# A decoder block on one core: tile-by-tile waits for reused bytes, and value loads queued behind the exchanged queries

## The chip, the cores and the metric

The kernel runs on one core of a Trainium2 chip. The metric is the device time of one execution in microseconds (us); three runs of the kernel before took 944.96, 946.88 and 947.32 us, so the median is 946.88 us.

## The reference

The block normalizes `x` (1024 positions by 1024 channels, float32), projects it with `w_in`, runs two causal attentions side by side, multiplies each with a SiLU gate, projects both back, merges them with sigmoid gates, applies `w_out`, a second RMS norm and the residual.

```python
h = rms_norm(x, g_pre); proj = h @ w_in            # qa ka va fa za | qb kb vb zb | gates
ya = fox_attention(qa, ka, va, log_sigmoid(fa + b_forget))   # 8 heads of 64, decay by cumulated log_f
yb = diff_attention(rope(qb), rope(kb), vb, lam)             # 4 heads, 2 score maps of 64, values of 128
ya = ya * silu(za);  yb = rms_norm(yb, g_subln) * (1 - lam_init) * silu(zb)
merged = sigmoid(gate_a) * (ya @ w_branch[0]) + sigmoid(gate_b) * (yb @ w_branch[1])
out = x + rms_norm(merged @ w_out, g_post)
```

## The kernel before

Matmuls run on float32 operands that are split in a rounded high part and a low remainder, so one product is two or three matmuls. The work has four stages in the program's order.

- **Values first.** The eight row blocks of `x` are normalized and transposed into `hT`; all value projections (`v_block`) and the forget gates are computed, split, and written to device memory (`va_d`, `vb_d`).
- **Attention, eight units.** Units 0 to 3 are the four differential heads, units 4 to 7 pairs of forgetting heads. `unit_proj(u)` makes four tasks, each a 128x512 projection of 24 matmuls (`project`, L246): k and q, each in two chunks, named `pk` and `pq`. In units 0 to 3 every chunk goes through `rope`: ACT copies the PSUM tile to `raw` (L283), SP issues four DMAs that swap 32-row bands into `sw` (L287; `swk`, `swq`), DVE multiplies and adds (L288, L290), POOL multiplies the swapped copy (L289). `stack` then makes the stacked operands `TA`, `TB`, `KA`, `KB` with two ACT casts (L295, L297) and two DVE subtractions (L296, L298). `swapped` (L407) fetches, for a group of two query blocks, the half-exchanged queries `X0` and `X1` by two DMAs each. `s_row` makes a row of scores: matmuls with the stacked queries (L421) and with the exchanged ones (L422), into one of three PSUM buffers, and DVE reduces each piece (L423), which frees the buffer. ACT takes the exponential (L428), POOL scales and adds (L512, L515). `av` transposes the probabilities (L450), splits them (L453, L454) and multiplies with the values (L474).
- **How units overlap.** While unit u runs its scores, the projections of unit u+1, the gate projections `z` and other small tasks are its filling work. The projections have two PSUM buffers (`pj`). The values of a unit are one load of 1 MB (`V`, L495) into one of two buffers; `load()` stands at the start of the unit.
- **Gates, merge, output.** `h_load` fetches eight 1 MB tiles `T`, `gates_plain` and `gates_pair` compute the merge gates, `branch` and `merge` the two back projections, `out_pair` the output.

A scheduler sets the order of the instructions on each engine from the program's order as priority, from the dependences, and from modelled durations. Every engine then runs its own list in order. All DMAs stand in the one list of SP, which stops at the first DMA that has to wait. Pools are memory areas: a pool opened over the bytes of a closed one has to wait for them.

Of the kernel before, what the change touches and what calls it, by code (L numbers as in the profile page):

```python
# [21 lines left out]
CH = 512  # L22
# [19 lines left out]
def f32(ap):  # L42
    return ap.bitcast(F32)
# [3 lines left out]
def tile_hybrid_block(  # L47
# [18 lines left out]
    nc = tc.nc  # L66
# [41 lines left out]
    t_d = {m: [dram.tile([P, 4, CH], F32, name=f"t_d{m}_{part}") for part in range(2)]  # L108
           for m in (4, 5, 6, 7)}
# [139 lines left out]


    with ExitStack() as st:
        qk = st.enter_context(tc.tile_pool(name="qk", bufs=2))
        pp = st.enter_context(tc.tile_pool(name="pp", bufs=6))
        ptp = st.enter_context(tc.tile_pool(name="ptp", bufs=3))
        stg = st.enter_context(tc.tile_pool(name="stg", bufs=2))
        pj = st.enter_context(tc.tile_pool(name="pj", bufs=2, space=PSUM))
        sps = st.enter_context(tc.tile_pool(name="sps", bufs=3, space=PSUM))
        tps = st.enter_context(tc.tile_pool(name="tps2", bufs=2, space=PSUM))
        yps = st.enter_context(tc.tile_pool(name="yps", bufs=1, space=PSUM))

        nc.sync.dma_start(gsub, g_subln.rearrange("o p -> p o"))
        nc.gpsimd.tensor_scalar(gsub, gsub, 1.0 - LAM_INIT, 1.0, op0=ALU.mult, op1=ALU.mult)
# [138 lines left out]
        def swapped(T, m, g, nm):  # L401

            src = T["TB" if m else "TA"]
            qs = slice(2 * g * P, (2 * g + 2) * P)
            t = qk.tile([P, 2 * P], F32R, tag=f"X{m}", name=f"X{m}{nm}_{g}", bufs=3)
            for a, b in ((UPR, DNR), (DNR, UPR)):
                nc.sync.dma_start(f32(t[a]), f32(src[b, qs]))  # L407
            return t

        def s_row(T, m, i, X, bias, boff, nm):  # L410

# [73 lines left out]
        def unit_attn(u, T):  # L485

            diff = u < 4
            t = u if diff else u - 4
            vt = qk.tile([P, NB, 256], F32R, tag="V", name=f"V{u}")
            src = (vb_d if diff else va_d)[:, t, :].rearrange("(b p) c -> p b c", p=P)  # L490
            cb = []
            groups = []

            def load():
                nc.sync.dma_start(f32(vt), src)  # L495
# [36 lines left out]
            else:  # L532
# [25 lines left out]
                for g in GORD[u]:  # L558
                    for m in range(2):
# [4 lines left out]
                            lambda m=m, g=g, rows=rows: av(  # L564
                                rows, g, vt, m * P, True, evac(m, g), f"f{u}_{m}_{g}",
                                u == 7 and g in FING)))
            return load, groups


        lt = pp.tile([P, 4, 64], F32, tag="P", name="lt")  # L570
# [43 lines left out]
        T, tasks = unit_proj(0)  # L614
        for tk in tasks:
            tk()
        pend = None
        for u in range(8):
            load, groups = unit_attn(u, T)
            if u == 1:  # L620
                forget_sums()
            load()
            fill = []
            if u + 1 < 8:
                T, tasks = unit_proj(u + 1)
                fill += tasks
            for t in ZFILL[u]:
                fill += z_tasks(t)
            fill[2:2] = [lambda k=k: h_combinations(k) for k in TFILL[u]]
            for t in SFILL[u]:  # L630
                fill += [lambda t=t, c=c: sum_squares(t, c) for c in range(2)]
                fill.append(lambda t=t: subln_scales(t))
            total = sum(s[0] for s in groups)
            done, nf = 0, 0
            for n, (wgt, rws, prd) in enumerate(groups):
                for r in rws:
                    r()
# [14 lines left out]


    gw = ExitStack()
    wx = gw.enter_context(tc.tile_pool(name="wx", bufs=2))
    tmp = gw.enter_context(tc.tile_pool(name="tmp", bufs=8))
    ydp = gw.enter_context(tc.tile_pool(name="ydp", bufs=1))
    xst = ExitStack()
    xps = xst.enter_context(tc.tile_pool(name="xps", bufs=8, space=PSUM))

    def split(dst, src, eng=nc.vector):

# [82 lines left out]


    tst = ExitStack()
    tpool = tst.enter_context(tc.tile_pool(name="tpool", bufs=1))

    yz = {}  # L750

# [36 lines left out]
             for m, (kh, sh) in hB.items()}  # L788

    def h_load():  # L790
        for m in (4, 6, 5, 7):
            ts = [tpool.tile([P, 4, CH], F32R, tag=f"T{m}{part}", name=f"T{m}{part}")
                  for part in range(2)]
            for part in range(2):
                nc.sync.dma_start(f32(ts[part]), t_d[m][part])
            h_ops[m] = [[t[:, k, :] for k in range(4)] for t in ts]

    def gates_pair(d, order):
        raw = []
# [19 lines left out]
    tst.close()  # L819


    mpool = gw.enter_context(tc.tile_pool(name="mpool", bufs=1))
# [205 lines left out]
```

## Time and profile before

| what | value |
|---|---|
| median of three runs | 946.88 us |
| the profiled execution: its time / its span | 945.37 us / 943.3 us |
| PE busy | 895.5 us, 95% of the span |
| DVE, ACT, POOL busy | 625.4, 435.8, 489.3 us |
| mean granted clock of TensorE | 0.988 |
| values first / attention / the rest, from the span's start | about 0 to 113, 113 to 603, 603 to 943 us |

The page gives busy times per engine; a table of stretches gives them for any part of the span, with the granted clock (1.00 is full speed) and what the DMA engines moved. Rows of the timeline start with the start and the duration in us; in brackets stands how long the engine was idle before and what ended that. "pk", "pq", "Sd" and so on are names of tiles without their numbers.

### The profile page before, as it was taken

The numbers are of one execution on the slowest core, as the hardware profiler recorded it, in microseconds if no ns is written. First come the engines' busy times: TensorE is split into PE (matmuls) and PEld (weight loads), VectorE is DVE, ScalarE is ACT, GpSimd is POOL, SyncE is SP. The second block draws the span as 40 slices with busy tenths as digits, with TensorE's granted clock in tenths as the row PEclk, the third lists the DMA queues.
The fourth block names the chain that finished last, engine by engine and source line by source line (L and its number), as shares of the span: only waits on it lengthen the run. The fifth ranks groups of instructions, "written<-read, shape, count | busy, mean of one in ns | idle before, by whom it ended". The sixth has DMA issues, their size and how long they took to land. (4 is left out here: it accounts for less than half of the span.)

```text
span 943.3 us, 13785 instructions
## 1 busy us (share of the span) xinstructions
PE 895.5 (95%) x4600; PEld 750.5 (80%) x4600; DVE 625.4 (66%) x1180; ACT 435.8 (46%) x862; POOL 489.3 (52%) x461
## 2 busy tenths in 40 slices
PE   7999989999999999999999998899999999999993
PEld 5899868787887888888878887788888888887872
DVE  6731248988767778577767558515868893559766
ACT  3421115575656766465755648524443450324331
POOL 7200024446546448364554566407667436878963
PEclk9999999999999999999999999999999999999997
DMA  9532354424316163444542442496556596211332
GB/s 312 186 129 90 118 151 121 110 74 120 108 42 196 43 181 126 123 125 138 167 151 74 135 151 92 152 404 234 174 176 196 165 351 222 72 40 46 105 118 89
DMA packets 118664, 136.95 MB, mean 145 GB/s; under 512 B 10545, under 2 KB 84273, under 8 KB 117570
## 3 DMA queue, kind: packets, MB, share of 16 engines
q1 hardware_dynamic: 118594, 136.08, 45.6%
q8 instruction: 36, 0.59, 0.3%
q14 instruction: 34, 0.28, 0.1%
HBM read 85.65 MB, written 37.81 MB: 131 GB/s over the span
## 5 line engine op out<-in xcount | busy, mean ns | idle before, releaser
L195 PE MATMUL pv<-wvhi,hT 128*128 128x264 f32 (+2 forms) x384 | 89.6, 326 | 0.4 <-DVE hT L181 0.4
L246 PE MATMUL pk<-hT,hi_k 128*128 128x512 f32 x256 | 84.8, 404 | 4.0 <-DVE KB L298 2.2
L246 PE MATMUL pz<-hT,hi_z 128*128 128x512 f32 x256 | 84.3, 396 | 0.0
L246 PE MATMUL pq<-hT,hi_q 128*128 128x512 f32 x256 | 82.8, 397 | 0.0
L713 PE MATMUL x_o<-wo_op,a_o 128*128 128x512 f32 x336 | 77.9, 391 | 3.6 <-POOL a_o L665 2.3
L846 PE MATMUL pb<-yT,hi_br 128*128 128x512 f32 x256 | 78.5, 389 | 0.0
L713 PEld LDWEIGHTS x_o<-wo_op,a_o 128*128 128x128 f32 x336 | 62.7, 188 | 18.7 <-POOL a_o L665 3.7
L713 PE MATMUL x_g<-T,a_g 128*128 128x512 f32 x336 | 77.5, 389 | 0.0
L713 PEld LDWEIGHTS x_g<-T,a_g 128*128 128x128 f32 x336 | 63.1, 188 | 13.1
L195 PEld LDWEIGHTS pv<-wvhi,hT 128*128 128x128 f32 x384 | 64.7, 191 | 6.3 <-DVE hT L181 0.7
L542 POOL TENSOR_SCALAR Pf<-Pf,lf 128x1024 f32<-128x1024 f32 (+3 forms) x64 | 52.5, 822 | 30.6 <-DVE lf L430 27.5
L428 ACT ACTIVATE Pf<-Pf,mxf 128x1024 f32<-128x1024 f32 (+3 forms) x64 | 49.7, 777 | 31.3 <-DVE mxf L423 28.8
L428 ACT ACTIVATE Pd<-Pd,mxd 128x128 f32<-128x128 f32 (+7 forms) x64 | 49.5, 774 | 30.8 <-DVE mxd L423 29.1
L538 POOL TENSOR_TENSOR cb<-cb,trim 128x128 f32<-128x128 f32 x64 | 30.2, 474 | 61.8 <-DVE mxf L423 44.2
L195 PE MATMUL pv<-wvlo,hT 128*128 128x512 f32 (+2 forms) x192 | 61.9, 325 | 0.0
L512 POOL TENSOR_SCALAR Pd<-Pd,ld 128x128 f32<-128x128 f32 (+7 forms) x32 | 25.5, 798 | 69.7 <-DVE ld L511 37.8
L246 PEld LDWEIGHTS pk<-hT,hi_k 128*128 128x128 f32 x256 | 48.3, 193 | 14.5 <-DVE KB L298 2.4
L713 PE MATMUL x_g<-hT,a_g 128*128 128x512 f32 x252 | 58.6, 389 | 0.0
L454 DVE TENSOR_TENSOR plf<-ptf,phf 128x512 fp32r<-128x512 f32 (+1 forms) x80 | 49.6, 633 | 10.4 <-ACT phf L453 9.8
L846 PEld LDWEIGHTS pb<-yT,hi_br 128*128 128x128 f32 x256 | 48.1, 188 | 10.0
L713 PEld LDWEIGHTS x_g<-hT,a_g 128*128 128x128 f32 x252 | 47.3, 188 | 9.8
L246 PEld LDWEIGHTS pq<-hT,hi_q 128*128 128x128 f32 x256 | 47.5, 189 | 8.9
(248 smaller groups left out, 2424.4 us busy)
## 6 DMA issues: line engine op xcount, KB each, us to landing
t_d<-t SPq DMA_DIRECT2D x32, 256.0 KB, 2.2
T<-t_d SPq DMA_DIRECT2D x8, 1024.0 KB, 14.9
raw<-in_w_in_dram SPq DMA_DIRECT2D x14, 512.0 KB, 4.1
vb_d<-vbs SPq DMA_DIRECT2D x8, 512.0 KB
va_d<-vas SPq DMA_DIRECT2D x8, 512.0 KB, 3.7
raw_k<-in_w_in_dram SPq DMA_DIRECT2D x8, 512.0 KB, 5.3
raw_q<-in_w_in_dram SPq DMA_DIRECT2D x8, 512.0 KB
V<-vb_d SPq DMA_DIRECT2D x4, 1024.0 KB
```

Of the source, the lines that this page charges most:

```text
L195: nc.tensor.matmul(ps[n], lhsT=hT[hp][k // 4][i // 4][:, k % 4, hs], rhs=wt[k][:, a:b], start=first, stop=(k == KT - 1 and hp == 1))
L246: nc.tensor.matmul(ps, lhsT=a[:, k, :], rhs=hT[h][k // 4][c][:, k % 4, :], start=(k == 0 and a is hi and h == 0), stop=(k == KT - 1 and a ...
L428: nc.scalar.activation(pr[:, 0:n], pr[:, 0:n], AF.Exp, bias=mx[:, len(pcs) - 1:len(pcs)], scale=-1.0, accum_out=le)
L454: nc.vector.tensor_tensor(pl[:, 0:n], pt[:, 0:n], ph[:, 0:n], op=ALU.subtract)
L512: nc.gpsimd.tensor_scalar(p2[:, 0:n], p2[:, 0:n], l2, 1.0, op0=ALU.mult, op1=ALU.mult)
L538: nc.gpsimd.tensor_tensor(diag, diag, trim, op=ALU.add)
L542: nc.gpsimd.tensor_scalar(p1[:, 0:n], p1[:, 0:n], l1, 1.0, op0=ALU.mult, op1=ALU.mult)
L713: nc.tensor.matmul(x[m], lhsT=a[:, ai, k, :], rhs=right[m][bi][k], start=(k == 0 and n == 0), stop=(k == 3 and n == 2))
L846: nc.tensor.matmul(ps, lhsT=a[:, kk, :], rhs=yT[g][h][:, k % 2, sl], start=(k == 0 and a is hi and h == 0), stop=(k == 3 and a is lo))
```

## The change

Three things are changed together.

1. The pools of attention and of what follows are opened with `reuse_waits="tile"`: where such a pool lies over the bytes of a closed one, each of its tiles waits only for the tiles that held its own bytes, and no longer for the whole closed pool. Several pools are laid from the other end of the memory (`side="right"`).
2. `h_load` allocates its tiles in the order 6, 4, 7, 5 and loads them in the order 4, 6, 5, 7 as before.
3. The load of a unit's values leaves `load()`. `load_v` is put in the list `vload`, and `swapped` issues it right behind the first DMA pair it makes after that: for unit 0 behind its first `X0`, for each later unit behind the first exchanged queries that are fetched once half of the groups of the unit before it have been traced.

```diff
-        qk = st.enter_context(tc.tile_pool(name="qk", bufs=2))
-        pp = st.enter_context(tc.tile_pool(name="pp", bufs=6))
...
+        qk = st.enter_context(tc.tile_pool(name="qk", bufs=2, reuse_waits="tile"))
+        pp = st.enter_context(tc.tile_pool(name="pp", bufs=6, side="right", reuse_waits="tile"))
...
+        pj = st.enter_context(tc.tile_pool(name="pj", bufs=2, space=PSUM, reuse_waits="tile"))
...
             for a, b in ((UPR, DNR), (DNR, UPR)):
-                nc.sync.dma_start(f32(t[a]), f32(src[b, qs]))
+                lastx[0] = nc.sync.dma_start(f32(t[a]), f32(src[b, qs])).ins
+            if vload:
+                with tc.issue_after(lastx[0]):
+                    vload.pop(0)()
             return t
+
+        lastx, vload = [None], []
...
+            def load_v():
+                nc.sync.dma_start(f32(vt), src)
+
             def load():
-                nc.sync.dma_start(f32(vt), src)
...
-            return load, groups
+            return load, load_v, groups
...
+        nxt = None
         for u in range(8):
-            load, groups = unit_attn(u, T)
+            load, load_v, groups = nxt or unit_attn(u, T)
+            nxt = None
+            if u == 0:
+                vload.append(load_v)
...
             for n, (wgt, rws, prd) in enumerate(groups):
+                if n == len(groups) // 2 and u < 7:
+                    nxt = unit_attn(u + 1, T)
+                    vload.append(nxt[1])
...
-    xps = xst.enter_context(tc.tile_pool(name="xps", bufs=8, space=PSUM))
+    xps = xst.enter_context(tc.tile_pool(name="xps", bufs=8, space=PSUM, reuse_waits="tile"))
...
-    tpool = tst.enter_context(tc.tile_pool(name="tpool", bufs=1))
+    tpool = tst.enter_context(tc.tile_pool(name="tpool", bufs=1, reuse_waits="tile"))
...
     def h_load():
+
+        ts = {m: [tpool.tile([P, 4, CH], F32R, tag=f"T{m}{part}", name=f"T{m}{part}")
+                  for part in range(2)] for m in (6, 4, 7, 5)}
         for m in (4, 6, 5, 7):
-            ts = [tpool.tile([P, 4, CH], F32R, tag=f"T{m}{part}", name=f"T{m}{part}")
-                  for part in range(2)]
             for part in range(2):
-                nc.sync.dma_start(f32(ts[part]), t_d[m][part])
-            h_ops[m] = [[t[:, k, :] for k in range(4)] for t in ts]
+                nc.sync.dma_start(f32(ts[m][part]), t_d[m][part])
+            h_ops[m] = [[t[:, k, :] for k in range(4)] for t in ts[m]]
```

In the changed kernel the lines L421 to L454 become L426 to L459, the value load L495 becomes L500, and the `T` loads L795 become L810. No instruction is added or taken out. The order of the engines differs from shortly before the attention to the first groups of unit 4, then is the same up to the seam at the gates, where the DMAs stand in another order. Three places follow.

**SP, the start of unit 0, before.** `V0` and `V1` are the values of units 0 and 1, `raw_q1` a weight load of 0.5 MB for unit 1, `swk0_0` and `swq0_0` the band swaps of unit 0's first chunks.

```order
L211 DMA va_d_97<-vas7_1116 128x1024
L572 DMA lt_1160<-in_lambda_q2_dram 128x64
L572 DMA lt_1160<-in_lambda_k2_dram 128x64
L495 DMA V0_1345<-vb_d_96 128x8x256
L495 DMA V1_1912<-vb_d_96 128x8x256
L228 DMA raw_q1_1514<-in_w_in_dram 128x8x128
L287 DMA swk0_0_1210<-rawk0_0_1208 32x512 x4
L287 DMA swq0_0_1255<-rawq0_0_1253 32x512 x4
L287 DMA swk0_1_1294<-rawk0_1_1292 32x512 x4
L407 DMA X0d0_0_1351<-TA0_1173 64x256 x2
L407 DMA X1d0_0_1354<-TB0_1174 64x256 x2
L287 DMA swq0_1_1333<-rawq0_1_1331 32x512 x4
```

The same place in the changed kernel:

```order
L211 DMA va_d_97<-vas7_1116 128x1024
L228 DMA raw_q1_1514<-in_w_in_dram 128x8x128
L287 DMA swk0_0_1210<-rawk0_0_1208 32x512 x4
L287 DMA swq0_0_1255<-rawq0_0_1253 32x512 x4
L287 DMA swk0_1_1294<-rawk0_1_1292 32x512 x4
L407 DMA X0d0_0_1350<-TA0_1173 64x256 x2
L500 DMA V0_1345<-vb_d_96 128x8x256
L407 DMA X1d0_0_1354<-TB0_1174 64x256 x2
L287 DMA swq0_1_1333<-rawq0_1_1331 32x512 x4
```

`V0` has moved from ahead of the first swaps to between `X0` and `X1` of unit 0's first group; `V1` stands eight rows below, between `X0` and `X1` of the third group and ahead of `swq1_0`. The four small loads `lt` stand about ten rows higher. The loads of the later units stand where they stood, within four rows.

**DVE, the second half of unit 0, before.** `lo_z0` is the low part of a gate weight, `TA1` a stacked query of unit 1, L423 the reduction of a piece of scores (listed as ISA).

```order
L290 TENSOR_TENSOR rawq1_0_1545<-rawq1_0_1545,swq1_0_1547 128x512
L423 ISA Pd0_0_4_1565,mxd0_0_4_1566<-Sd0_0_4_1_1571,dmask_1157,mxd0_0_4_1566 128x256
L423 ISA mxd0_0_4_1566 128x1
L236 TENSOR_TENSOR lo_z0_1853<-raw_z0_1850,hi_z0_1852 128x1024
L296 TENSOR_TENSOR TA1_1347<-rawq1_0_1545,TA1_1347 64x512
L423 ISA Pd0_1_4_1578,mxd0_1_4_1579<-Sd0_1_4_0_1580,dmask_1157 128x384
```

In the changed kernel (L428 is the reduction there):

```order
L296 TENSOR_TENSOR TA1_1346<-rawq1_0_1545,TA1_1346 64x512
L298 TENSOR_TENSOR TB1_1347<-rawq1_0_1545,TB1_1347 64x512
L428 ISA Pd0_0_4_1567,mxd0_0_4_1568<-Sd0_0_4_1_1573,dmask_1157,mxd0_0_4_1568 128x256
L428 ISA mxd0_0_4_1568 128x1
L236 TENSOR_TENSOR lo_z0_1855<-raw_z0_1852,hi_z0_1854 128x1024
L435 RECIPROCAL ld0_1_3_1489<-ld0_1_3_1489 128x1
L435 RECIPROCAL ld0_0_4_1577<-ld0_0_4_1577 128x1
L518 TENSOR_TENSOR ld0_1_3_1489<-ld0_1_3_1489,nlam_83 128x1
L428 ISA Pd0_1_4_1580,mxd0_1_4_1581<-Sd0_1_4_0_1582,dmask_1157 128x384
```

`TA1` now stands ahead of the reduction before `lo_z0`, so that between two reductions of scores `lo_z0` is the one long operation left. On PE, the same shift has put more filling work ahead: before the first score matmul of unit 1 stand 3 matmuls of unit 2's first projection in the kernel before, and 17 in the changed one.

**PE, the seam at the gates, before** (with what each row waits for; `pg` is the first gate projection):

```order
L474 MATMUL ypf_1_0_6860<-phf_1_0_0_6862,V_6170 128x256 [waits Activation_49]
L474 MATMUL ypf_1_0_6860<-plf_1_0_0_6863,V_6170 128x256 [waits DVE_49]
L474 MATMUL ypf_1_0_6860<-phf_1_0_0_6862,V_6170 128x128
L474 MATMUL ypf_1_0_6860<-plf_1_0_0_6863,V_6170 128x128
L246 MATMUL pg_0_0_6923<-hT_88,hi_g_0_6919 128x512 [waits DVE_49]
```

In the changed kernel:

```order
L479 MATMUL ypf_1_0_6860<-phf_1_0_0_6862,V_5934 128x256 [waits Activation_49]
L479 MATMUL ypf_1_0_6860<-plf_1_0_0_6863,V_5934 128x256 [waits DVE_49]
L479 MATMUL ypf_1_0_6860<-phf_1_0_0_6862,V_5934 128x128
L479 MATMUL ypf_1_0_6860<-plf_1_0_0_6863,V_5934 128x128
L246 MATMUL pg_0_0_6923<-hT_88,hi_g_0_6919 128x512
```

The first gate matmul has lost its wait for DVE. On SP, the eight `T` loads stand there ahead of four `yd` loads and two loads of `x`, and before behind them.

More of the change, by code (lines that the diff above doesn't have):

```diff
@@ L251, in tile_hybrid_block @@
     with ExitStack() as st:
-        qk = st.enter_context(tc.tile_pool(name="qk", bufs=2))
-        pp = st.enter_context(tc.tile_pool(name="pp", bufs=6))
[L254 to L259, printed above, removed]
+        qk = st.enter_context(tc.tile_pool(name="qk", bufs=2, reuse_waits="tile"))
+        pp = st.enter_context(tc.tile_pool(name="pp", bufs=6, side="right", reuse_waits="tile"))
+        ptp = st.enter_context(tc.tile_pool(name="ptp", bufs=3, side="right", reuse_waits="tile"))
+        stg = st.enter_context(tc.tile_pool(name="stg", bufs=2, side="right", reuse_waits="tile"))
+        pj = st.enter_context(tc.tile_pool(name="pj", bufs=2, space=PSUM, reuse_waits="tile"))
+        sps = st.enter_context(tc.tile_pool(name="sps", bufs=3, space=PSUM, reuse_waits="tile"))
+        tps = st.enter_context(tc.tile_pool(name="tps2", bufs=2, space=PSUM, reuse_waits="tile"))
+        yps = st.enter_context(tc.tile_pool(name="yps", bufs=1, space=PSUM, reuse_waits="tile"))
         nc.sync.dma_start(gsub, g_subln.rearrange("o p -> p o"))
@@ L654, in tile_hybrid_block @@
     gw = ExitStack()
-    wx = gw.enter_context(tc.tile_pool(name="wx", bufs=2))
-    tmp = gw.enter_context(tc.tile_pool(name="tmp", bufs=8))
-    ydp = gw.enter_context(tc.tile_pool(name="ydp", bufs=1))
+    wx = gw.enter_context(tc.tile_pool(name="wx", bufs=2, side="right", reuse_waits="tile"))
+    tmp = gw.enter_context(tc.tile_pool(name="tmp", bufs=8, side="right", reuse_waits="tile"))
+    ydp = gw.enter_context(tc.tile_pool(name="ydp", bufs=1, side="right", reuse_waits="tile"))
     xst = ExitStack()
-    xps = xst.enter_context(tc.tile_pool(name="xps", bufs=8, space=PSUM))
+    xps = xst.enter_context(tc.tile_pool(name="xps", bufs=8, space=PSUM, reuse_waits="tile"))
     def split(dst, src, eng=nc.vector):
@@ L819, in tile_hybrid_block @@
     tst.close()
-    mpool = gw.enter_context(tc.tile_pool(name="mpool", bufs=1))
+    mpool = gw.enter_context(tc.tile_pool(name="mpool", bufs=1, reuse_waits="tile"))
     mg = mpool.tile([P, KT, S], F32, name="mg")
```

## The prediction

> **What bounds the kernel now.** I read the page's first part, then a table of stretches, then the waits of PE and the timeline around them.
>
> ```profile
> span 943.3 us, 13785 instructions
> PE 895.5 (95%) x4600; PEld 750.5 (80%) x4600; DVE 625.4 (66%) x1180; ACT 435.8 (46%) x862; POOL 489.3 (52%) x461
> ```
>
> PE is busy for 895.5 of 943.3 us. An order change removes no matmul, so only PE's idle 47.8 us and slow-clock time can be won. The stretches say where they lie.
>
> ```profile
> core 0: us, PE busy (x) PEld busy (x) DVE busy (x) ACT busy (x) POOL busy (x), PEclk, DMA share, GB/s
> 134.00:139.00 5.00, 1.19 (x5) 0.66 (x5) 4.88 (x6) 3.17 (x6) 0.70 (x1) 1.00 0.20 50
> 139.00:146.00 7.00, 7.00 (x28) 5.77 (x27) 6.74 (x10) 1.54 (x3) 2.95 (x3) 0.76 0.35 86
> 146.00:168.00 22.00, 21.71 (x105) 17.36 (x104) 18.71 (x43) 13.65 (x33) 12.14 (x13) 1.00 0.48 117
> 168.00:174.00 6.00, 4.09 (x13) 3.23 (x13) 5.87 (x15) 3.06 (x7) 1.30 (x2) 0.72 0.30 70
> 174.00:200.00 26.00, 25.52 (x136) 21.45 (x134) 23.95 (x50) 17.02 (x30) 16.24 (x12) 1.00 0.45 121
> 200.00:310.00 110.00, 104.57 (x557) 86.98 (x558) 84.07 (x208) 66.75 (x138) 55.94 (x46) 1.00 0.38 105
> 604.00:930.00 326.00, 320.32 (x1404) 262.96 (x1404) 211.39 (x224) 114.99 (x192) 206.79 (x141) 1.00 0.54 180
> ```
>
> Two stretches stand out: 134 to 139, where PE works 1.19 of 5 us, and 168 to 174. Behind each stop the granted clock is low (0.76 over 7 us, 0.72 over 6 us), so a stop is paid twice. After 604 PE works 320.32 of 326 us; what PE gains earlier is kept there. The timeline of PE gives the stops, and the seam at the gates.
>
> ```profile
> 128.25 0.39 PE L246 MATMUL pk<-hT,lo_k 128*128 128x512 f32 x1
> ...
> 133.69 0.39 PE L246 MATMUL pq<-hT,lo_q 128*128 128x512 f32 x1
> 135.84 0.70 PE L246 MATMUL pk<-hT,hi_k 128*128 128x512 f32 x2 [1.76 <-ACT rawk L283]
> 138.59 0.51 PE L246 MATMUL pk<-hT,lo_k 128*128 128x512 f32 x1 [2.04 <-DVE lo_k L236]
> ...
> 170.02 0.49 PE L421 MATMUL Sd<-KA,TA 128*128 128x256 f32 x1 [1.91 <-DVE mxd L423]
> ...
> 603.91 0.74 PE L246 MATMUL pg<-hT,hi_g 128*128 128x512 f32 x2 [0.91 <-DVE ys L552]
> ```
>
> Why PE stops at 134 is read backwards through four engines.
>
> ```profile
> 114.67 1.41 SPq L495 DMA_DIRECT2D V<-vb_d  x2
> 117.87 2.37 SPq L228 DMA_DIRECT2D raw_q<-in_w_in_dram  x1
> 120.33 4.68 SPq L287 DMA_DIRECT2D swk<-rawk  x4
> ...
> 130.16 0.69 DVE L288 TENSOR_TENSOR rawk<-rawk,cosT 128x512 f32<-128x512 f32 x1 [8.77 <-DMA swk<-rawk]
> 130.20 1.80 POOL L289 TENSOR_TENSOR swk<-swk,sinT 128x512 f32<-128x512 f32 x1 [19.21 <-DMA swk<-rawk]
> 133.83 0.62 ACT L295 CAST KA<-rawk 64x512 fp32r<-64x512 f32 x1 [10.01 <-DVE rawk L290]
> 135.11 0.59 ACT L283 COPY rawk<-pk 128x512 f32<-128x512 f32 x1
> ```
>
> The four swaps of the first k chunk are issued from 120.33 and have landed only at 130.16. DVE stands idle 8.77 us. ACT waits for the rotated chunk until 133.83, and behind its two casts in ACT's list stands the copy at 135.11 that empties the PSUM buffer PE needs next. Then DVE, late too, delays `lo_k` and PE once more. What held the swaps is the traffic ahead of them:
>
> ```profile
> 122.00:124.00 2.00, 2.00 (x11) 1.65 (x10) 0.00 (x0) 0.59 (x1) 0.00 (x0) 1.00 1.09 346
> 126.00:128.00 2.00, 2.00 (x10) 1.67 (x9) 0.00 (x0) 0.00 (x0) 0.00 (x0) 1.00 1.04 160
> ```
>
> First the two value loads (2.1 MB) at some 346 GB/s, 6.1 us; then `raw_q` (0.52 MB, pieces of 512 bytes) at some 160 GB/s, 3.3 us. The DMA engines are full in both.
>
> **The change part by part.**
>
> *Values behind the queries.* V0 and V1 leave the place ahead of `raw_q`. The swaps still follow `raw_q`, whose issue at 117.87 waits for DVE, not for V. What they then need:
>
> ```profile
> raw_k<-in_w_in_dram SPq DMA_DIRECT2D x8, 512.0 KB, 5.3
> ...
> swk<-rawk SPq DMA_DIRECT2D x32, 64.0 KB, 2.0
> ```
>
> ```profile
> 123.23 0.59 ACT L283 COPY rawq<-pq 128x512 f32<-128x512 f32 x1 [2.23 <-PE pq L246]
> ...
> 133.22 1.49 POOL L234 TENSOR_SCALAR hi_k<-raw_k 128x1024 fp32r<-128x1024 f32 x1
> ...
> 135.72 2.41 SPq L287 DMA_DIRECT2D swk<-rawk  x4
> ...
> 137.32 1.22 DVE L236 TENSOR_TENSOR lo_k<-raw_k,hi_k 128x1024 fp32r<-128x1024 f32 x1
> ```
>
> A weight load of this size takes 5.3 us from issue to landing, so `raw_q` lands at 123.2 and the swaps behind it at about 124.5 (estimate) instead of 130.16: 5.7 us earlier. The rotation takes 3.7 us as before (130.16 to 133.83), so ACT is free for the next copy when its chunk is done (PE's row at 128.25), over 4 us before PE asks at 133.9. The q swaps are issued once ACT has copied their chunk at 123.8, 2.4 us for four, and land 2.0 later, 128.3; POOL needs 1.8 for them and 1.5 for `hi_k`, DVE 1.2 for `lo_k`: 132.8, against 134.3 when PE asks. So the first stop goes: 5.00 − 1.19 = 3.81 us idle, and 7.00 × (1 − 0.76) = 1.7 us of slow clock. Sum 5.5 us, close to DVE's head start of 5.7. Bounds: nothing if `raw_q` alone holds the swaps, 5.7 if DVE's head start reaches PE whole. I take 5.5.
>
> *The second stop.* DVE is the late one here:
>
> ```profile
> 165.35 2.31 DVE L236 TENSOR_TENSOR lo_z<-raw_z,hi_z 128x1024 fp32r<-128x1024 f32 x1 [0.54 <-POOL hi_z L234]
> 167.70 1.67 DVE L296 TENSOR_TENSOR TA<-rawq,TA 64x512 fp32r<-64x512 f32 x1
> 169.40 0.56 DVE L423 CUSTOM_DVE_ANT_0 Pd<-Sd,dmask 128x384 f32<-128x384 f32 x1
> ```
>
> `lo_z` and `TA` together keep DVE 4.05 us from the reduction that frees a score buffer. In the new order `TA` stands ahead of the reduction before, so 1.67 of the 1.91 us go by order alone, and DVE comes 5.7 us early. If the stop goes, so does the slow clock, 6.00 × (1 − 0.72) = 1.7 us: 3.6 us. Lower bound 0, since DVE is busy 18.71 of 22 us before it and may be late again. I take 3.6.
>
> [...]
>
> *The price of the new place.* V0 (1 MB, 3.0 us at 346 GB/s) now passes ahead of `X1` of the first group and of the second chunk's q swaps, V1 ahead of `X1` of the third group. By the times above `X0` is issued at about 133, V0 ends at 139.6, `X1` lands at 140, the swaps at 140.7. In PE's new order 24 + 9 projection matmuls stand ahead of the first product with `X1`; at 0.23 us each (326 us / 1404 in the gates) PE reaches it at 142. DVE waits for the swaps a microsecond or so, with PE's filling work as cover. So 0; if the cover is short, up to 3.0 us per load and the clock behind it.
>
> *What is given back.* DVE's own work is unchanged, and 14 more filling matmuls stand ahead of unit 1's first scores: 14 × 0.23 = 3.2 us of cover used early. In units 0 to 3 PE still idles 5.4 us (200 to 310) and mostly for DVE's reductions:
>
> ```profile
> PE Sd L421 <- DVE mxd L423: 4.0, 9, 1.0
> ```
>
> (174 to 385: 4.0 us in nine waits, longest 1.0.) From unit 4 on the order is the same, so nothing is won or lost there. Between 0 and 3.2 I take half, 1.6 us.
>
> *Tile-by-tile waits.* At the seam the first gate matmul no longer waits for the last DVE result: 0.9 us (row at 603.91). The eight T loads can start some 7 us earlier, but PE runs full from 604 on, so they are worth 0. At the first seam the long wait of the page,
>
> ```profile
> POOL hi_k L234 <- DMA vb_d<-vbs: 48.3, 1, 48.3
> ```
>
> belongs to a pool that is not changed and is covered by the value projections: 0. The `lt` loads move off DVE's list, where they only fill its idle time: 0. Issue costs: the same number of DMAs.
>
> *Sum:* 5.5 + 3.6 + 0.9 − 1.6 = 8.4 us. Against the profiled execution, 945.4 us (span 943.3 and 2.1 around it), that is 937.0; against the median of the runs, 946.9, it is 938.5. I predict 938.
>
> **The rivals.**
>
> - *DVE takes most of it back.* The first stop goes, but the second stays and the whole 3.2 us are given back: −5.5 − 0.9 + 3.2 = −3.2, about 943. For it: DVE busy 23.95 of 26 us after 174. Against it: the new place of `TA`.
> - *The values now stop PE (slower).* `X1` and the swaps behind V0 and V1 come after PE's cover is used up. Each such stop costs 3.0 us and, as behind the 1.91 us stop, 1.7 us of clock: 2 × 4.7 = 9.4. With the second stop left as it is: −5.5 − 0.9 + 9.4 = +3.0, about 949.5. It decides from the point where the first `X1` lands later than about 142 in today's time. For it: the swaps at 130.16 came only after everything issued ahead of them. [...] Against it: 2 us of margin, and a single load instead of two.
> - *The first stop doesn't go,* since `raw_q` with its 512-byte pieces still stands ahead of the swaps: only the 0.9 us of the seam, about 946. Against it: the 6.1 us that V took by the rate.
> - *More is won:* half of the waits in 200 to 310 go too, nothing is given back: 8.4 + 1.6 + 2.7 = 12.7, about 933.5.
>
> **How the numbers follow.** Chances: forecast 0.60 (its own range 934 to 941), DVE takes back 0.20, values stop PE 0.08, no first stop won 0.08, more won 0.04. The range has to leave out at most 0.2: 932 to 945 holds the forecast, the DVE rival and the larger gain, and leaves out 0.16. Three tenths of a per cent is about what a measurement of this kernel can tell from no change, here 2.8 us, so "faster" is below 944.0. Faster: 0.60 + 0.04 + 0.12 of the DVE rival = 0.76; same: 0.08 + 0.08 = 0.16; slower 0.08.
>
> **What would show it.** In the changed kernel's profile the first `swk` lands near 124, ACT's copy of the second k chunk ends before 131, PE has no stop over 1 us between 113 and 145 and the clock stays 1.00 there. No stop by L428 over 1 us with a low clock behind it around 160. The first `pg` follows the last `ypf` without a gap, at about 595 to 596. T is issued at about 594 to 600. I am wrong if PE stops for `X1` (L427) or if stops for L428 in units 0 to 3 sum to more than 8 us.

## The result, and the profile after

The changed kernel takes 937.73 us (median of 4 runs, 936.16 to 939.74), the kernel before in the same session 947.1 us (4 runs). The ratio is 0.9905, 95% interval 0.9878 to 0.9932: faster by 9.4 us, beyond what counts as no change. A second session, shown below, gave 0.9919 (0.9900 to 0.9938). Slow executions are left out of all medians: there is one, of 1102 us at a clock of 0.85, in the experiment with one more load. The profiled execution took 938.31 us, 7.06 less than the profiled one before. The head of its page:

```profile
span 936.2 us, 13774 instructions
PE 891.2 (95%) x4600; PEld 746.8 (80%) x4600; DVE 627.0 (67%) x1180; ACT 437.1 (47%) x862; POOL 493.6 (53%) x461
```

The table of stretches of the changed kernel, with the columns shown before (length, busy time and count of PE, PEld, DVE, ACT, POOL, then PE's granted clock, the DMA share, GB/s):

```profile
134.00:139.00 5.00, 4.49 (x22) 3.58 (x21) 4.80 (x6) 1.24 (x2) 1.48 (x2) 1.00 0.42 124
139.00:146.00 7.00, 6.25 (x29) 4.96 (x28) 2.82 (x7) 1.37 (x4) 1.78 (x1) 1.00 0.71 192
146.00:168.00 22.00, 20.57 (x94) 15.52 (x94) 19.17 (x52) 14.80 (x33) 12.06 (x12) 1.00 0.67 174
168.00:174.00 6.00, 5.74 (x30) 4.73 (x28) 5.26 (x5) 2.21 (x4) 5.81 (x5) 1.00 0.59 155
174.00:200.00 26.00, 22.25 (x114) 17.86 (x115) 22.37 (x52) 15.55 (x27) 13.07 (x9) 1.00 0.31 84
200.00:310.00 110.00, 107.48 (x584) 90.69 (x584) 89.75 (x222) 71.44 (x152) 58.87 (x49) 1.00 0.39 107
```

The hole at 134 to 139 (PE 1.19 of 5 us before) is nearly closed and the clock is full through 174. But 174 to 200, where PE was busy for 25.52 us, now has 22.25. PE's timeline of the changed kernel shows which waits are left. The number in square brackets is the idle time ahead of the row.

```profile
136.16 0.30 PE L426 MATMUL Sd<-KB,TB 128*128 128x128 f32 x1 [0.51 <-DVE TB L298]
142.64 0.30 PE L427 MATMUL Sd<-KB,X1d 128*128 128x128 f32 x1 [0.75 <-DMA X1d<-TB]
...
163.09 0.50 PE L426 MATMUL Sd<-KA,TA 128*128 128x512 f32 x1 [0.84 <-DVE mxd L428]
...
176.34 0.44 PE L426 MATMUL Sd<-KA,TA 128*128 128x384 f32 x1 [0.82 <-DVE mxd L428]
...
199.50 0.60 PE L615 MATMUL ft<-ident,fs 128*8 128x128 f32 x4 [1.77 <-DVE fs L606]
...
595.37 0.27 PE L479 MATMUL ypf<-plf,V 128*128 128x128 f32 x1
595.48 0.68 PE L246 MATMUL pg<-hT,hi_g 128*128 128x512 f32 x2
```

No stop between 113 and 146 is longer than 0.75 us; what stops PE now are reductions (at 163, 174, 176 and 193) and the transposes of the forget gates (`ft`, fed by `fs`); the first gate matmul `pg` follows the last value product without a gap. SP's queue and DVE in the changed kernel, for the chain that the prediction followed backwards:

```profile
116.11 0.38 SPq L228 DMA_DIRECT2D raw_q<-in_w_in_dram  x1
117.37 2.53 SPq L287 DMA_DIRECT2D swk<-rawk  x4
...
134.59 1.15 SPq L407 DMA_DIRECT2D X0d<-TA  x2
135.79 0.58 SPq L500 DMA_DIRECT2D V<-vb_d  x1
136.46 1.22 SPq L407 DMA_DIRECT2D X1d<-TB  x2
137.78 2.44 SPq L287 DMA_DIRECT2D swq<-rawq  x4
```

```profile
121.51 0.69 DVE L288 TENSOR_TENSOR rawk<-rawk,cosT 128x512 f32<-128x512 f32 x1 [5.43 <-DMA swk<-rawk]
128.32 0.69 DVE L288 TENSOR_TENSOR rawq<-rawq,cosT 128x512 f32<-128x512 f32 x1 [2.15 <-DMA swq<-rawq]
...
143.44 0.69 DVE L288 TENSOR_TENSOR rawq<-rawq,cosT 128x512 f32<-128x512 f32 x1 [3.00 <-DMA swq<-rawq]
```

The first k swaps land at 121.51 instead of 130.16. The second q swaps, now behind V0, let DVE wait 3.00 us.

How far the changed kernel is ahead at the same point of the work, from the timelines of PE (start of the row; "again" is the second profiled execution of the same kernel, from the last set of runs below):

| point | before | changed | again | lead |
|---|---|---|---|---|
| first `pq` | 116.66 | 116.55 | 116.05 | 0.1 / 0.6 |
| last `ypd` (end of unit 3) | 383.88 | 378.64 | 376.81 | 5.2 / 7.1 |
| the stop at `pk` by `KB` | 489.98 | 483.37 | 481.16 | 6.6 / 8.8 |
| last `ypf` | 602.73 | 595.37 | 592.11 | 7.4 / 10.6 |
| first `pg` | 603.91 | 595.48 | 592.22 | 8.4 / 11.7 |
| span | 943.3 | 936.2 | 932.2 | 7.1 / 11.1 |

At the last `ypd` the two kernels have not done the same work: PE has 1979 matmuls behind it in the changed kernel and 1972 in the kernel before. Seven matmuls at 364.51 / 1972 = 0.185 us are 1.3 us, so the lead in work is nearer 6.5 and 8.4 us there, and it hardly changes from there to the stop at `pk`.

### The profile page after: what moved, and what is told of

Its sections match the earlier page's. It is cut to its first block, busy times and chain, and to the rows that moved or that the text cites. A ratio compares the mean times of both kernels' runs of the same rounds, so it can differ in the third digit from the quotient of the medians.

```text
span 936.2 us, 13774 instructions
## 1 busy us (share of the span) xinstructions
PE 891.2 (95%) x4600; PEld 746.8 (80%) x4600; DVE 627.0 (67%) x1180; ACT 437.1 (47%) x862; POOL 493.6 (53%) x461
## 5 line engine op out<-in xcount | busy, mean ns | idle before, releaser
L246 PE MATMUL pk<-hT,hi_k 128*128 128x512 f32 x256 | 81.1, 394 | 2.0 <-DVE KB L298 2.0
L549 POOL TENSOR_SCALAR Pf<-Pf,lf 128x1024 f32<-128x1024 f32 (+3 forms) x64 | 50.4, 790 | 28.3 <-DVE lf L435 23.9
L459 DVE TENSOR_TENSOR plf<-ptf,phf 128x512 fp32r<-128x512 f32 (+1 forms) x80 | 49.8, 634 | 10.9 <-ACT phf L458 10.2
```

The source lines that it names most:

```text
L246: nc.tensor.matmul(ps, lhsT=a[:, k, :], rhs=hT[h][k // 4][c][:, k % 4, :], start=(k == 0 and a is hi and h == 0), stop=(k == KT - 1 and a ...
L459: nc.vector.tensor_tensor(pl[:, 0:n], pt[:, 0:n], ph[:, 0:n], op=ALU.subtract)
L549: nc.gpsimd.tensor_scalar(p1[:, 0:n], p1[:, 0:n], l1, 1.0, op0=ALU.mult, op1=ALU.mult)
```

## The experiments

The theory was: the value loads' place makes the gain, by way of the swaps and DVE; the pools add the seam; what is lost again in units 0 to 3 is DVE's lateness. The rivals: the tile-by-tile waits carry the gain; `raw_q`, not the values, holds the swaps (see *V0 at the front*); the losses come from POOL or from the place of `fs`. Each set of four ran on one chip beside the kernel before, whose medians were 944.64, 943.54 and 943.94 us.

### The values alone, the pools alone

*The values alone.* To the kernel before, only `load_v`, `vload` and `issue_after` are added; pools and `T` stay as they were:

```diff
+            if vload:
+                with tc.issue_after(lastx[0]):
+                    vload.pop(0)()
...
             def load():
-                nc.sync.dma_start(f32(vt), src)
```

> Only the value loads are moved; every pool and the T tiles are as before. Theory (the place of the value loads makes the gain, the pools add only the seam at the gates): the order on PE up to the gates is that of the changed kernel, so the first k swaps land near 121.5, PE has no stop over 1 us between 113 and 146, and the first gate matmul again starts about 0.9 us behind the last value product. Time about 1 us over the changed kernel: 938 to 940, ratio 0.991 to 0.993. Rival (the tile-by-tile waits of the unit pools carry part of it): a stop over 1 us is back before 174, ratio 0.995 or more.

Measured: 938.45 us, ratio 0.9924 (0.9905 to 0.9944). The first k swaps land at 122.79, PE idles 0.33 us in 113 to 146, and the seam is there again. PE's timeline of this kernel:

```profile
161.51 0.50 PE L426 MATMUL Sd<-KA,TA 128*128 128x512 f32 x1 [1.46 <-DVE mxd L428]
...
198.69 0.60 PE L615 MATMUL ft<-ident,fs 128*8 128x128 f32 x4 [2.58 <-DVE fs L606]
...
596.86 0.74 PE L246 MATMUL pg<-hT,hi_g 128*128 128x512 f32 x2 [0.91 <-DVE ys L559]
```

The values make most of the gain, 944.64 − 938.45 = 6.2 us. The rival's sign, a stop over 1 us ahead of 174, was there too (1.46 us), but without its price.

*The pools alone.* The changed kernel with the value loads back in `load()`:

```diff
             def load():
+                load_v()
...
-            if u == 0:
-                vload.append(load_v)
...
-                    nxt = unit_attn(u + 1, T)
-                    vload.append(nxt[1])
```

> All pools and the T tiles as in the changed kernel, the value loads at the start of their unit as before. In this kernel's list on SP, V0 and V1 stand ahead of the first k swaps, but raw_q of unit 1 stands behind them. Theory (the swaps land when all that is issued ahead of them is through): V0 and V1 are issued at about 114 to 115 and take 6.1 us, so the swaps land at about 122 to 123 instead of 130.16; most of the first stop goes without any move of the values, and PE's stops between 113 and 146 sum to under 2 us. Ratio 0.993 to 0.997. Rival (it is the values themselves ahead of the swaps that make the stop): swaps after 127, stops of 3 us or more at 134 to 139, only the 0.9 us of the seam is won, ratio 0.998 to 1.000.

Measured: 941.61 us, 0.9966 (0.9951 to 0.9981). The pools alone win 3 us, by more than the seam. SP's queue and POOL in this kernel:

```profile
110.25 1.00 SPq L500 DMA_DIRECT2D V<-vb_d  x2
```

```profile
123.33 1.55 POOL L289 TENSOR_TENSOR swk<-swk,sinT 128x512 f32<-128x512 f32 x1 [12.07 <-DMA swk<-rawk]
```

V0 and V1 are issued at 110.25 instead of 114.67, the DMA engines move 312 GB/s in 115 to 120 and 51 in 120 to 125, and the swaps land at 123.33; PE idles 1.6 us in 113 to 146. So the theory holds (what stands ahead of the swaps counts, not the values as such), with a cause that I had not seen: the pools move the values out of the way by themselves. More than half of what is won up to 146 is lost again behind it, where PE idles 11.0 us up to 385 (8.4 before).

### The seam

The changed kernel with `wx`, `tmp`, `ydp`, `xps`, `tpool`, `mpool` and the `T` loads as before:

```diff
-    xps = xst.enter_context(tc.tile_pool(name="xps", bufs=8, space=PSUM, reuse_waits="tile"))
+    xps = xst.enter_context(tc.tile_pool(name="xps", bufs=8, space=PSUM))
```

> The changed kernel with the pools of the last stages (weights and temporaries of the gates, their PSUM pool, T, the merge) and the T loads as before. Theory (the seam at the gates is worth 0.9 us and nothing else): the first gate matmul starts 0.7 to 1.1 us behind the last value product, PE runs without a gap from there as in the changed kernel, ratio 0.9905 to 0.9925, that is 0.9 us over the changed kernel. Rival one (the earlier T loads help the gates too): 2 us or more over the changed kernel. Rival two (the seam is worth nothing since the gates wait elsewhere): no difference to the changed kernel, the gap is made up by 751.

Measured: 936.96 us, 0.9922 (0.9909 to 0.9935). In the profile the first `pg` (595.15) waits 0.91 us by `ys` again. From the last `ypf` to the first `pg` it is 1.18 us here, 1.18 before and 1.19 with the values alone, against 0.11 in the changed kernel and with the pools alone: the seam is worth 1.07 us. The whole time does not resolve it against the changed kernel (0.9905 and 0.9919).

### Where V0 stands

*V0 at the front,* all else as changed:

```diff
             if u == 0:
-                vload.append(load_v)
+                load_v()
```

> The changed kernel with the load of V0 back at the start of unit 0, ahead of the first k swaps; V1 and the later values stay behind X. raw_q of unit 1 stands behind the swaps here. Theory (3.0 us of V0 are hidden in front of the swaps, whose predecessor raw_q is gone): the swaps land at 120 to 122, no stop over 1 us before 146, and the wait of 0.75 us for X1 and DVE's 3.0 us for the second q swaps, both behind V0 in the changed kernel, go. Ratio 0.988 to 0.992, within 1.5 us of the changed kernel. Rival (V0 ahead of the swaps brings half of the first stop back): a stop of 1 to 2 us at 134 to 139 with a slow clock behind it, ratio 0.994 or more.

Measured: 933.76 us, 0.9880 (0.9862 to 0.9899). SP's queue of this kernel, and DVE's row:

```profile
109.75 0.37 SPq L500 DMA_DIRECT2D V<-vb_d  x1
...
117.32 2.53 SPq L287 DMA_DIRECT2D swk<-rawk  x4
119.90 0.58 SPq L228 DMA_DIRECT2D raw_q<-in_w_in_dram  x1
```

```profile
121.51 0.69 DVE L288 TENSOR_TENSOR rawk<-rawk,cosT 128x512 f32<-128x512 f32 x1 [2.11 <-DMA swk<-rawk]
```

V0 is issued at 109.75, when nothing waits for the queue (SP's next issue is at 112.08); the swaps land as early as in the changed kernel, and nothing stops for `X1`. `raw_q` stands behind the swaps here and ahead of them in the changed kernel, and they land at 121.51 in both: `raw_q`, issued 1.3 us ahead of them, doesn't hold them there. PE idles 7.3 us in 146 to 385 instead of 8.8.

*V0 at the front with the old pools:* the same edit on the kernel with the values alone.

> Pools and T as before; V1 and the later values behind X, V0 at the start of unit 0. V0 then waits, as in the kernel before, behind the loads of lt until about 114.7 (with the tile-by-tile waits it was issued at 109.75), and raw_q of unit 1 stands between it and the swaps. Theory (it is the early issue that makes V0 free at the front): V0's 3.0 us and raw_q's 3.3 us stand ahead of the swaps, they land at 123.5 to 126, and the time is between 0.9925 and 0.995 of before. Rival (any place of V0 will do once V1 is away): ratio 0.987 to 0.991 as with V0 at the front and the new pools.

Measured: 938.42 us, 0.9945 (0.9930 to 0.9959). SP's queue and DVE:

```profile
114.56 0.45 SPq L579 DMA_DIRECT2D lt<-in_lambda_k_dram  x1
115.11 0.38 SPq L500 DMA_DIRECT2D V<-vb_d  x1
118.32 0.38 SPq L228 DMA_DIRECT2D raw_q<-in_w_in_dram  x1
```

```profile
126.75 0.69 DVE L288 TENSOR_TENSOR rawk<-rawk,cosT 128x512 f32<-128x512 f32 x1 [5.13 <-DMA swk<-rawk]
```

V0 stands behind the last `lt` load and is issued 5.4 us later than with the new pools, `raw_q` follows it, and the swaps land 5.2 us later. The time is longer than with V0 at the front and the new pools, and the intervals of the two ratios do not meet. But up to 146 the later swaps cost PE little: it idles 0.89 us here and 0.67 there. At the last `ypd`, with 1972 matmuls done in both, this kernel is 3.5 us behind (378.19 against 374.72), at the last `ypf` 7.4 (595.91 against 588.51), with the stop at `pk` by `KB` in between (1.96 us), which the other has not. So the two parts of the change work on the same place, but that the later landing of the swaps makes the whole difference is not shown.

*One more load ahead of the swaps,* on the kernel before (`V0`'s bytes into two unused tiles, between V0 and V1):

```diff
                 nc.sync.dma_start(f32(vt), src)
+                if u == 0:
+                    for n in range(2):
+                        x = pp.tile([P, 4, 256], F32, tag="P", name=f"vx{n}")
+                        nc.sync.dma_start(x, src[:, 4 * n:4 * n + 4].bitcast(F32))
```

> The kernel before with one more load of 1 MB, the bytes of V0 a second time into two unused tiles, issued between V0 and V1, so ahead of raw_q and the first k swaps. Theory (the swaps wait for all traffic ahead of them): they land some 3.0 us later than in the kernel before, at about 133, and PE's stops at 134 to 142 grow from 3.8 to 6.5 us or more; time 2 to 4 us above before, ratio 1.002 to 1.005. Rival (raw_q with its pieces of 512 bytes holds the swaps, not the values): the swaps land within 1 us of 130.16, and the time is that of before, ratio 0.999 to 1.001.

Measured: 944.38 us, 1.0005 (0.9990 to 1.0019). DVE's row and the stretch 113 to 146 of this kernel, then that stretch of the kernel before:

```profile
133.48 0.69 DVE L288 TENSOR_TENSOR rawk<-rawk,cosT 128x512 f32<-128x512 f32 x1 [11.61 <-DMA swk<-rawk]
```

```profile
113.00:146.00 33.00, 28.18 (x112) 22.15 (x111) 14.21 (x18) 5.02 (x9) 7.76 (x5) 0.90 0.63 180
```

```profile
113.00:146.00 33.00, 28.57 (x119) 22.68 (x118) 16.70 (x24) 6.26 (x11) 7.45 (x6) 0.95 0.50 142
```

The swaps land 3.3 us later, as the theory had it. Up to 146 PE loses 4.82 us idle and 33 × 0.10 = 3.3 us of clock, 8.1 together, against 4.43 + 1.65 = 6.1 before: 2.0 us more. Only 0.4 us of that is idle time, the rest is the clock of one execution. At the last `ypd` this kernel is behind by 2.3 us (386.16 against 383.88) and by 11 matmuls (1961 against 1972). It makes that up later: the kernel before has a stop of 1.98 us and a slow clock there (0.83 over 490 to 500), and this one's order has no such stop.

```profile
489.98 0.73 PE L246 MATMUL pk<-hT,hi_k 128*128 128x512 f32 x2 [1.98 <-DVE KB L298]
```

By the last `ypf` the two are 0.3 us apart (603.06 and 602.73), and the total shows nothing. So the landing is shown to follow the traffic, and one profile shows the lateness up to the end of unit 3. The price in the total, which the theory had at 2 to 4 us, is missed: an order that changes all the way can win back elsewhere what it loses here.

*The values behind X1* (and so behind the second q swaps):

```diff
-            if vload:
+            if vload and (m or not nm.startswith('d')):
```

> The changed kernel with each of the differential units' value loads behind the second tile of exchanged queries (X1) of its group instead of the first (X0); on SP V0 then stands behind the q swaps of the second chunk too. Theory (V0 ahead of X1 and of the swaps costs what the trace shows, PE's 0.75 us and part of DVE's idle 3.0 us): no stop by X1, DVE waits under 1.5 us for the second q swaps, 0.5 to 1.5 us below the changed kernel, ratio 0.989 to 0.991. Rival (the cover was there, the 0.75 us are chance): time within 0.5 us of the changed kernel. Rival two (V0 is now late for its first product): PE stops for V before 165, ratio over 0.992.

Measured: 935.47 us, 0.9920 (0.9894 to 0.9946), no difference to the changed kernel, so the rival holds. DVE no longer waits for the second q swaps at all, PE idles 0 in 113 to 146, but 10.0 us in 146 to 385. DVE's wait behind V0 was covered, as predicted.

### What is given back

*The forget sums at unit 0.*

```diff
-            if u == 1:
+            if u == 0:
                 forget_sums()
```

> The changed kernel with the forget sums (the fs operations on DVE, two transposes ft on PE) called at unit 0 instead of unit 1. Theory (what is given back in 174 to 200 comes from DVE, whose small fs operations wait for POOL's additions: 1.84 us instead of 0.2 for one of 128x64 beside a POOL addition): the stop of 1.77 us by fs goes, DVE's list from 190 to 202 is free of them, and at about 140, where DVE stands idle 3.0 us for the second q swaps, they cost PE under 0.5 us. Time 1.5 to 3.5 us below the changed kernel, ratio 0.987 to 0.989. Rival (the stop only moves: fs with ACT's two table loads now stands in front of the rotation of the second chunk): a stop of 1.5 us or more by fs or by DVE between 135 and 165, ratio 0.990 or more.

Measured: 939.12 us, 0.9944 (0.9926 to 0.9962), not faster than the changed kernel (their intervals overlap, the median is higher), whose stop of 1.77 us is gone. PE's timeline has another in its place:

```profile
174.78 0.50 PE L426 MATMUL Sd<-KA,TA 128*128 128x512 f32 x1 [1.80 <-DVE mxd L428]
```

PE idles 10.6 us in 146 to 385. The theory fell: with the stop at `ft` gone, another of the same size stands where DVE is late.

*V0 at the front and the forget sums at unit 0.*

> V0 loaded at the start of unit 0, ahead of the first k swaps, and the forget sums called at unit 0; all else as in the changed kernel. Theory (DVE's work in units 0 and 1 is what is left): PE busy in 146 to 310 rises by 1 us or more against the kernel with V0 at the front alone, ratio 0.985 to 0.988. Rival (with V0 at the front PE does not stop for fs any more, so there is nothing to win, and fs ahead of the rotation can only cost): ratio 0.988 to 0.991.

Measured: 931.24 us, 0.9866 (0.9848 to 0.9885). PE's idle time in 146 to 385 is 5.6 us. The total does not show that the forget sums' place helps, since the interval overlaps that of V0 at the front alone. PE's rows show where a gain goes: at the last `ypd`, with 1972 matmuls done in both, this kernel is 2.8 us ahead (371.94 against 374.72), and by the last `ypf` it is 0.4 us behind (588.89 against 588.51). It has the stop at `pk` by `KB` in between (2.00 us), which the order with V0 at the front alone has not.

*No addition on POOL.* This kernel leaves out the sum of the two softmax parts in units 0 to 3.

```diff
-                    nc.gpsimd.tensor_tensor(
-                        p1[:, 0:n], p1[:, 0:n], p2[:, 0:n], op=ALU.add)
                     rows[i] = p1
```

> The changed kernel without POOL's addition of the two weighted softmax parts of a row in units 0 to 3 (the second part is computed and then left out). Theory (POOL's additions, up to 2.4 us each, hold DVE's two-input and small operations, and so make the reductions late that PE waits for): DVE operations of 128x64 take no more than 0.6 us, and PE's idle time in 146 to 385 falls from 8.8 us to under 5; 3 to 6 us below the changed kernel, ratio 0.984 to 0.987. Rival (DVE's own work sets the reductions): idle time within 1.5 us of 8.8, ratio 0.989 to 0.992.

Measured: 929.29 us, 0.9847 (0.9829 to 0.9865), 5.8 us below the changed kernel of the same set. The stretch 146 to 385, first of the changed kernel (its second profile), then without the addition:

```profile
146.00:385.00 239.00, 229.22 (x1227) 191.94 (x1226) 190.95 (x452) 148.71 (x301) 133.07 (x113) 1.00 0.43 120
```

```profile
146.00:385.00 239.00, 231.54 (x1258) 196.00 (x1257) 179.48 (x464) 152.55 (x308) 81.53 (x81) 1.00 0.44 122
```

DVE gets more operations done in the stretch (464 against 452) and is busy 11.5 us less. One group of it (changed kernel, same profile; then without the addition):

```profile
L236 DVE TENSOR_TENSOR lo_q<-raw_q,hi_q 128x1024 fp32r<-128x1024 f32 x4 | 8.3, 2086 | 1.6 <-POOL hi_q L234 1.6
```

```profile
L236 DVE TENSOR_TENSOR lo_q<-raw_q,hi_q 128x1024 fp32r<-128x1024 f32 x4 | 5.6, 1405 | 0.0
```

That mean alone doesn't show the cause, since with V0 at the front and the additions kept it is 1398 ns. But in the first profile of the changed kernel, in the same stretch, the eight `lo` operations of 128x1024 (`lo_q`, `lo_k`, `lo_z`) that have no POOL operation beside them took 1.21 to 1.23 us, and the five that overlap an addition, some of them another POOL operation as well, 1.60 to 3.13. So POOL's additions do lengthen DVE's work. Still, PE's idle time falls by 2.3 us only (9.8 to 7.5), within the rival's bound, and one `fs` operation of 128x64 takes 1.10 us here, where the theory allowed 0.6. The total falls as the theory said, but that doesn't prove it: this order does not have the stop at `pk` by `KB` (1.93 us in the changed kernel's second profile), and that is more than half of the 3.4 us by which it is ahead at the last `ypf` (588.74 against 592.11). POOL's part in DVE's work is shown; how much of the 5.8 us is due to it is not, and most of PE's idle time in 146 to 385 stays without it.

### The changed kernel and the best one, side by side

> The changed kernel once more, beside the three others of this set. Ratio 0.989 to 0.993. Its profile shows what is chance between executions of one order: if the 0.75 us stop for X1 at 142 and the place of the slow clock after 380 were the order's, they come again; if they were the execution's, they do not.

Measured: 935.11 us, 0.9919 (0.9900 to 0.9938). DVE and the stretch 113 to 146 in this profile:

```profile
126.27 0.69 DVE L288 TENSOR_TENSOR rawq<-rawq,cosT 128x512 f32<-128x512 f32 x1 [0.58 <-DMA swq<-rawq]
```

```profile
113.00:146.00 33.00, 33.00 (x152) 27.48 (x151) 17.80 (x26) 9.48 (x20) 9.53 (x6) 1.00 0.48 128
```

The first q swaps, issued at 122.30 here and at 122.81 in the first profile, land at 126.27 here and at 128.32 there. With them `X0` is issued at 131.56 instead of 134.59, V0 at 132.76 instead of 135.79, and the stop for `X1` is not there. In one and the same order that stop belongs to the execution.

> V0 at the front and the forget sums at unit 0, once more, beside the changed kernel. Theory (V0 issued 5 us earlier runs while the queues are empty, and the fs operations stand where DVE and POOL have nothing else): 3 to 6 us below the changed kernel, ratio 0.985 to 0.988, PE idle in 146 to 385 between 5 and 7 us. Rival (the earlier difference was the session's): within 2 us of the changed kernel.

Measured: 931.55 us, 0.9870 (0.9851 to 0.9890), 3.6 us below the changed kernel, and the intervals do not meet. V0 at the front, the later values behind X, the new pools and the forget sums at unit 0 beat both kernels.

## Why the prediction was right, step by step

The predicted time was 938; measured 937.73, and by the second session's ratio 0.9919 × 946.9 = 939.2. The total was right, and in part by luck: a term that the sum had too high and gains that it did not have nearly cancel.

- **"So the first stop goes", 5.5 us: right.** In 134 to 146 the kernel before lost 3.81 us idle and 1.7 of clock. The changed kernel idles 1.26 us in its first profile and 0 in its second: 4.2 and 5.5 us won, with the clock at 1.00 and ACT's copy of the second k chunk at 127.63, ahead of 131.
- **"The swaps behind it at about 124.5": too late by 3 us.** They land at 121.51, and two steps failed. The first is "so `raw_q` lands at 123.2 and the swaps behind it at about 124.5", with `raw_q` "at some 160 GB/s, 3.3 us". The bytes say otherwise (an estimate by count): from 117 to 126 the DMA engines moved 9.00 us × 287 GB/s = 2.58 MB in the kernel before, about the two value loads and `raw_q` together (2.62 MB), so the stretch at 160 GB/s behind it carries the swaps. And V0 at the front, with `raw_q` behind the swaps, has them at 121.51 as well. The second is "the `lt` loads move off DVE's list, where they only fill its idle time: 0". It is worth 1.3 of the 3 us: with the values alone, where `lt` stands as before, the swaps land at 122.79. DVE in the kernel before, then in the changed one:

```profile
115.34 0.23 DVE L575 TENSOR_TENSOR lt<-lt 128x64 f32<-128x64 f32 x1 [3.06 <-DMA lt<-in_lambda_k_dram]
...
116.61 1.23 DVE L236 TENSOR_TENSOR lo_q<-raw_q,hi_q 128x1024 fp32r<-128x1024 f32 x1 [0.79 <-DMA va_d<-vas]
```

```profile
114.86 1.23 DVE L236 TENSOR_TENSOR lo_q<-raw_q,hi_q 128x1024 fp32r<-128x1024 f32 x1 [2.68 <-DMA va_d<-vas]
```

  `lo_q` stood behind the `lt` operation that waited for its load. `lo_q` frees the buffer that `raw_q` of unit 1 waits for, which is now issued at 116.11 instead of 117.87. PE's stop of 0.62 us at 117.89 by `lo_q` goes as well. It is there in all four profiles with the old unit pools (0.62, 0.33, 0.74, 0.61) and with the new ones 0.16 us at most: some 0.6 us that the sum had not.
- **"At the first seam ... 0": wrong when the pools are taken alone,** as the pools-alone run shows (V issued 4.4 us earlier, 0.9966). In the changed kernel it hardly counts, since the values have left that place.
- **"If the stop goes, so does the slow clock", the second stop, 3.6 us, and 1.6 us given back: the mechanism failed.** The stop at 170.02 is gone, but "1.67 of the 1.91 us go by order alone" did not shorten PE's waiting: it waits at 163, 174, 176, 193 and 199.5 instead. The stops by L428 in units 0 to 3 sum to 4.9 and 6.2 us (6.1 by L423 before), under the 8 us named as a sign of being wrong, but in the second profile no less than before. In 146 to 200 the kernel before lost 2.67 us idle and 54 × 0.03 = 1.6 us of clock, 4.3 together; the changed one 5.45 and 5.71 us in its two profiles. What it wins comes later: 200 to 385 idles 3.33 and 4.07 us instead of 5.69. Over 146 to 385 the net is some 1.2 and 0.2 us, where 3.6 − 1.6 = 2.0 was predicted. I had priced one stop by the row that showed it, though PE waits for the same engine at several places of the stretch.
- **"The price of the new place ... 0": right as a size, wrong in the margin.** DVE waited 3.00 and 2.56 us for the swaps behind V0, not "a microsecond or so", and still PE lost at most 0.75 us. "I am wrong if PE stops for X1" was the condition; it did in one of two profiles, for a quarter of the 3.0 us named as its price.
- **The seam, 0.9 us: right,** 1.07 by the rows. `pg` at 595.48 and `T` issued from 594.83 on are where they were expected.
- **"From unit 4 on ... nothing is won or lost": right for the order, wrong for a single execution.** Between the stop at `pk` and 521 the changed kernel gains 1.7 us (lead 6.6 to 8.3), since in the kernel before a slow clock (0.83 over 490 to 500) follows that stop and in the changed one none. Later it loses time to a slow spell of its own at 560 to 570 (0.83), which its second profile does not have (1.00).
- **"What PE gains earlier is kept there" (behind 604): nearly.** Of the lead at the first `pg`, 8.4 and 11.7 us, 7.1 and 11.1 are left at the end, so in the first profile the seam's 1.07 us is lost again.

Of the rivals, "DVE takes most of it back" was half true: it took back most or nearly all of the second stop, but not the first. Why one order of these three engines idles 5.6 us in 146 to 385 and another 11.0 stays open; POOL's additions are shown to lengthen DVE's work there (`lo` operations took 1.60 to 3.13 us beside one, 1.21 to 1.23 with no POOL operation beside them), and the place of `fs` alone is not the cause, since PE idles 10.6 us with it moved.

## What to carry to other kernels

A large load that nothing needs yet should go where the queue is empty, and that can be earlier as well as later: the values behind X made most of the 9 us, and V0 five us earlier, with the forget sums moved, 3.6 us more. Look for small loads and operations that wait at the head of an in-order list, since everything behind them waits as well: here `lo_q` started at 116.61 behind the `lt` operation, and at 114.86 without it. A stop removed from a stretch in which PE waits for the same engine again and again should be priced by the idle time of the whole stretch, not by its own row. And where an edit changes the order of everything behind it, compare the kernels at the same point of the work as well as by their totals: a stop far behind the edit came and went here with the order, at 2 us a time.

## What the runs showed of the hardware

**A small operation ended with a whole one of another engine.** With the pools alone, one `fs` operation of 128x64 on DVE took 4.02 us; its neighbours take 0.22. DVE, then POOL in that kernel:

```profile
198.68 4.02 DVE L604 TENSOR_TENSOR fs<-fs 128x64 f32<-128x64 f32 x1
202.74 0.22 DVE L605 TENSOR_TENSOR fs<-fs 128x64 f32<-128x64 f32 x1
```

```profile
199.04 2.36 POOL L523 TENSOR_TENSOR Pd<-Pd,Pd 128x1024 f32<-128x1024 f32 x1
201.37 1.25 POOL L289 TENSOR_TENSOR swk<-swk,sinT 128x512 f32<-128x512 f32 x1
```

It ends at 202.70, as POOL's second operation ends at 202.62, and PE then stops 3.11 us for `pld` behind it. It is recorded 0.36 us ahead of the first of POOL's two operations, the addition, and ends 0.08 us behind the second; why it spans both is not shown. The `lo` operations beside POOL's additions fit: in the changed kernel one took 3.13 us beside an addition of 2.11, where those with no POOL operation beside them took 1.21 to 1.23.

**The clock did not fall by the length of a stop.** With the seam as before, a stop of 1.43 us is followed by a clock of 0.66 (PE's row, then the stretch):

```profile
160.84 0.58 PE L426 MATMUL Sd<-KA,TA 128*128 128x512 f32 x1 [1.43 <-DVE mxd L428]
```

```profile
160.00:165.00 5.00, 4.17 (x11) 3.31 (x12) 4.82 (x13) 3.49 (x7) 2.56 (x3) 0.66 0.48 107
```

The stop of 2.58 us at 198.69 with the values alone is followed by none:

```profile
195.00:200.00 5.00, 2.42 (x13) 1.71 (x13) 4.62 (x7) 1.17 (x3) 3.75 (x3) 1.00 0.32 79
200.00:205.00 5.00, 5.00 (x31) 4.24 (x30) 3.14 (x4) 3.17 (x7) 1.01 (x1) 1.00 0.08 28
```

The spell costs 5.00 × (1 − 0.66) = 1.7 us, as the two in the prediction did. Whether one comes could not be read from the length of the stop here, so that a single stop should be charged with a part of 1.7 us, not the whole. What decides it is not shown.
